# A two-layer hybrid encoder on one core: lo parts by TensorE, a head norm per query, another order of the input projections, and other places for the down projection's operands

## The chip, the cores and the metric

The kernel runs on one core of one Trainium2 chip. The metric is the device time of one execution in microseconds (us), as the median of the runs of a kernel; lower is better.

## What is computed

The reference normalises x (1024 tokens of 1024 features, float32) and sends it through two layers. Cut to what matters, one layer is:

```python
def layer(x):
    proj = x @ w_in + b_in            # conv pair | q | k | v | memory q: 14 chunks of 128, and v of 512
    conv_out = silu(layer_norm(depthwise_conv(a * sigmoid(gate), 31 taps)))    # 256 features
    # 4 differential heads of 128 features, with a relative bias
    s1, s2 = q1 @ k1.T * scale + bias, q2 @ k2.T * scale + bias
    o = (softmax(s1) - lam * softmax(s2)) @ v
    diff_out = o * rsqrt(mean(o * o) + 1e-5) * norm_g * (1 - lam_init)
    mem_out = softmax(qm @ km.T) @ vm                 # 4 heads against 256 memory tokens
    mixed = concat(conv_out, diff_out, mem_out)
    x = layer_norm(ALPHA * x + mixed @ w_out + b_out)
    return layer_norm(ALPHA * x + square(relu(x @ w_up)) @ w_down)   # 4096 hidden features
```

## The kernel before

**Numbers.** Every float32 product is made of two-part operands: a hi part (rounded to the type that TensorE takes, `fp32r` in the trace) and a lo part, the source minus hi. `mm3` (L111) issues three matmuls per product: hi by hi, hi by lo, lo by hi. `split` (L92) makes the parts: hi by a copy on ACT (L97), lo by a subtraction on DVE or POOL (L100). `split_turned` (L199) is the other way to make the parts of a tile that lies in PSUM after TensorE transposed it: ACT copies hi out, TensorE adds `minus` (the negative identity) times hi onto the same PSUM bank, and ACT copies what is left out as lo (L207). Before the change it is used for half of the tiles of the embedding and of the next layer's input (`to_xt`).

**Stages.** The embedding's norm, with the relative bias table and the memory's keys and values for both layers beside it. Then for each layer:

- Input projections (`pj`, L113 to L115) by chunks of 128 columns and halves of 512 tokens, with weights fetched and split by `weight` (L103). The table `ORDER` (L45) gives the order of the steps: letters are chunks (A, gate, Q, K, M), `v` a half of the value projection (`v_ps`), `norm` the transposes `ct` of the convolved channels with their norm (L404), `out` the conv group's silu (`conv_out`, transposes `cz`), `attn:1` the first step of attention. The convolution itself is a chain of scalar_tensor_tensor operations on DVE (`acc`, L344).
- Attention, as a pipeline of 40 blocks of 128 queries in the order of `HEADS`. A block has `scores` (matmuls `sc`, L532; bias and row minimum by DVE, L535; exp by ACT, L537), `combine` (the two softmaxes joined on DVE, L555 to L558), `turn` (8 transposes into two PSUM banks `at`, L578, and the split into tiles `at`), and `values` for pairs of blocks (`o`). In `turn` the first bank of a block is split by ACT and DVE; for the second bank ACT copies the tile out (`av`, L585) and takes hi from that, and POOL makes the lo. After every four blocks of a head comes the head norm: ACT copies `om` out (L619), POOL squares it (DVE in the last head, L621), a 512-column matmul with the 128x128 matrix `ones` sums over the features for all partitions (`ms`, L623), four matmuls add the epsilon term (L626), ACT takes Ln and Exp, and POOL (DVE in the last head) does five operations of 128x512 (L632 to L636).
- Output projection (`wo_ps`, 48 matmuls for each of 8 token tiles), then residual, bias and layer norm (`ln_row`, L149; its statistics by two bn_stats and a bn_aggr on DVE), and the forms `x11`, `x21`, `x22`, `xt1` to `xt4` of the tiles (`turn_form`, L780), which the next stage needs since it multiplies 2x2 blocks by a scheme of 7 products.
- Up projection (`uz`, `uc`, `ud`, L873) with the activation, hidden forms written to DRAM.
- Down projection (`dz`, `db`, L1053): two groups of 7 products, 4 steps (q) in each, 4 token tiles in a step, 6 matmuls for each, 512 columns wide: 2 x 7 x 96 = 1344 matmuls a layer. `down_forms` makes two operands for a step: `wf`, which streams through TensorE, in the stage's own pool `pd`; and `hf`, whose 128x128 parts are loaded as weights, in the pool `wts`. In the last product of group 1 the loaded operand (`hl`) lies in `pd`; in the first product of group 0 the streamed operand of q = 0 and 1 lies in `big`.

**What sets the order.** A scheduler orders the instructions of each engine by their dependencies; the code's order and the pools' buffers bound it. SBUF's pools are stacked from the low end of a partition (`cst`, `big`, `wts`, `sm`, then the stage's pool, `pd` or `pu`) and from the high end (the attention's pools). PSUM has two double banks (`pa`: scores, out projection, half of the down products) and four single ones (`pb`: `at`, `o`, `ms`, `v_ps`, forms, the rest). Loads and stores are issued on SP's queue in order; `bias_rows` (L238) issues four stores of 1 MB that write a skewed copy of each head's bias row (`skew`), from which `attn_load` later reads `bt`. It is called right behind the embedding (L732).

## Time and profile before

| | |
|---|---|
| median of 3 runs | 2481.17 us (2481.14 the lowest) |
| profiled execution | 2482.02 us |
| its span on the core | 2480.2 us, of which PE is busy for 94% |
| embedding, memory keys and values | 0 to 81 us |
| attention of the first layer | 286 to 515 us |
| output projection | 515 to 617 us |
| up projection's start, late forms | 617 to 650 us |
| up projection, then down projection (from 977.5 us) | to about 1240 us |
| second layer's attention | 1484 to 1714 us |

One execution took 9299.67 us; the median is not touched by it. The profile is that of one execution, which took 0.85 us more than the median; 1.8 us of its time lie outside the span. The stages are those of the trace, with their borders read to a microsecond or two.

### The profile page before, as it was taken

Reading aid. Unit: us, or ns where it says so; the run is one execution under the profiler, and the core shown is the slowest. Engines: PE = TensorE matmul, PEld = TensorE weight load, DVE = VectorE, ACT = ScalarE, POOL = GpSimd, SP = SyncE. Lnnn points to the kernel's source line nnn. Section 1 sums busy time; section 2 is a strip of 40 time slices with the busy share of each in tenths; the row PEclk is TensorE's granted clock in tenths of the full one; section 3 lists DMA queues with packets and bytes.
Section 4 is the critical chain, followed back from the end, with each engine's and each line's share of the span. In section 5 each row is a group of like instructions: output and inputs, shape, how many; then the busy total and the mean of one; then the engine's idle time right before and its main releaser. Section 6 shows DMA issues by size and latency. Waiting matters only on the chain.

```text
span 2480.2 us, 30322 instructions
## 1 busy us (share of the span) xinstructions
PE 2321.3 (94%) x11256; PEld 1908.5 (77%) x11256; DVE 1893.9 (76%) x2598; ACT 1105.8 (45%) x1864; POOL 485.0 (20%) x350
## 2 busy tenths in 40 slices
PE   5899998899899999999999899888989999999997
PEld 3788777677688887888878787776768888788885
DVE  7499779969866566757788977897896656586769
ACT  5212387732455554333431137875145555433332
POOL 1124175821000000000042324683200000000002
PEclk9999999999999999999999999999999999999999
DMA  9433445142344449343332346432424444854232
GB/s 315 155 123 98 148 134 146 52 143 106 115 145 145 157 168 398 104 166 97 100 119 85 110 124 194 107 80 92 164 84 139 145 154 152 338 188 161 94 95 101
DMA packets 137740, 355.74 MB, mean 143 GB/s; under 512 B 14804, under 2 KB 31956, under 8 KB 130900
## 3 DMA queue, kind: packets, MB, share of 16 engines
q1 hardware_dynamic: 137592, 353.81, 42.7%
q8 instruction: 88, 1.44, 0.3%
q14 instruction: 60, 0.49, 0.1%
HBM read 240.47 MB, written 117.47 MB: 144 GB/s over the span
## 4 chain that ended last, share of the span: by engine, by line
PE 64%; DVE 27%; issue 4%; DMA 4%; ACT 2%; SPq 0%; DVEq 0%; ACTq 0%
PE uz L873 14%; PE db L1053 12%; PE dz L1053 10%; DVE acc L344 7%; PE uc L873 7%; PE ud L873 4%; DVE s L535 3%; DVE s L557 3%; PE pj L113 2%; PE pj L114 2%; PE pj L115 2%; DVE ast L556 1%; PE wo_ps L115 1%; DVE at L100 1%; PE wo_ps L114 1%
## 5 line engine op out<-in xcount | busy, mean ns | idle before, releaser
L1053 PE MATMUL db<-wf,hf 128*128 128x512 f32 x1344 | 319.6, 398 | 7.0 <-ACT wf L97 5.0
L1053 PEld LDWEIGHTS db<-wf,hf 128*128 128x128 f32 x1344 | 254.9, 190 | 69.1 <-ACT wf L97 6.7
L163 POOL TENSOR_TENSOR yd<-yd,l2g 128x1024 f32<-128x1024 f32 x6 | 14.7, 2442 | 1314.0 <-ACT yd L162 1314.0
L1053 PE MATMUL dz<-wf,hf 128*128 128x512 f32 x1152 | 269.7, 395 | 0.0
L97 ACT ACTIVATE hf<-hr 128x1024 fp32r<-128x1024 f32 x104 | 110.3, 1061 | 337.1 <-PE db L1053 182.3
L1053 PEld LDWEIGHTS dz<-wf,hf 128*128 128x128 f32 x1152 | 217.0, 188 | 50.6
L100 DVE TENSOR_TENSOR hf<-hr,hf 128x1024 fp32r<-128x1024 f32 x104 | 127.1, 1222 | 140.8 <-ACT hf L97 140.2
L97 ACT ACTIVATE wu<-wu_r 128x512 fp32r<-128x512 f32 (+1 forms) x192 | 131.0, 699 | 227.9 <-PE uc L873 95.5
L873 PE MATMUL uz<-xt,wu 128*128 128x512 f32 x768 | 189.8, 395 | 6.0 <-ACT wu L97 6.0
L873 PE MATMUL uz<-x,wu 128*128 128x512 f32 x768 | 191.0, 395 | 0.0
L344 DVE SCALAR_TENSOR_TENSOR acc<-u,pp,acc 128x1009 f32<-128x1009 f32 (+14 forms) x120 | 182.4, 1560 | 0.6
L114 PE MATMUL pj<-x_l,wf 128*128 128x512 f32 x448 | 176.8, 395 | 2.7 <-DVE x_l L100 2.7
L113 PE MATMUL pj<-x_h,wf 128*128 128x512 f32 x448 | 177.3, 397 | 0.4 <-ACT x_h L97 0.4
L100 DVE TENSOR_TENSOR wu<-wu_r,wu 128x512 fp32r<-128x512 f32 (+1 forms) x192 | 145.6, 776 | 39.8 <-ACT wu L97 39.4
L115 PE MATMUL pj<-x_h,wf 128*128 128x512 f32 x448 | 175.9, 393 | 0.0
L873 PEld LDWEIGHTS uz<-xt,wu 128*128 128x128 f32 x768 | 144.1, 188 | 40.3 <-ACT wu L97 6.5
L537 ACT ACTIVATE s<-s,ast 128x1024 f32<-128x1024 f32 x128 | 147.3, 1152 | 55.7 <-DVE ast L535 53.4
L873 PEld LDWEIGHTS uz<-x,wu 128*128 128x128 f32 x768 | 145.9, 190 | 31.8
L535 DVE CUSTOM_DVE_ANT_0 s<-sc,bt 128x1024 f32<-128x1024 f32 x128 | 153.7, 1213 | 10.7 <-PE sc L533 10.0
L100 DVE TENSOR_TENSOR wf<-wd,wf 128x1024 fp32r<-128x1024 f32 x112 | 138.0, 1235 | 26.2 <-ACT wf L97 19.2
L890 DVE TENSOR_TENSOR h<-u,uc 128x512 f32<-128x512 f32 x64 | 44.0, 688 | 144.7 <-PE uc L873 120.8
L532 PE MATMUL sc<-ks,qs 128*128 128x512 f32 x256 | 111.8, 437 | 21.3 <-DVE ast L535 21.1
(261 smaller groups left out, 5365.1 us busy)
## 6 DMA issues: line engine op xcount, KB each, us to landing
hr<-hd SPq DMA_DIRECT2D x224, 256.0 KB, 2.9
wu_r<-in_w_up SPq DMA_DIRECT2D x64, 512.0 KB, 4.2
hd<-hs SPq DMA_DIRECT2D x128, 256.0 KB, 2.4
wd<-in_w_down SPq DMA_DIRECT2D x64, 512.0 KB, 7.7
hd<-h SPq DMA_DIRECT2D x96, 256.0 KB, 2.2
ks<-kd SPq DMA_DIRECT2D x32, 512.0 KB, 11.5
wf_raw<-in_w_f SPq DMA_DIRECT2D x28, 512.0 KB, 4.3
qd<-stg SPq DMA_DIRECT2D x8, 1024.0 KB, 4.4
```

What stands on the lines that cost most here:

```text
L97: nc.scalar.activation(hi, src, AF.Copy)
L100: (lo_eng or nc.vector).tensor_tensor(lo, src, f(hi), op=ALU.subtract)
L113: nc.tensor.matmul(ps, lhsT=lhs[0], rhs=rhs[0], start=start, stop=False)
L114: nc.tensor.matmul(ps, lhsT=lhs[0], rhs=rhs[1], start=False, stop=False)
L115: nc.tensor.matmul(ps, lhsT=lhs[1], rhs=rhs[0], start=False, stop=stop)
L344: nc.vector.scalar_tensor_tensor(acc[:, c, a:b], u[:, c, a + t - PAD:b + t - PAD], pp[:, k:k + 1], acc[:, c, a:b], ALU.mult, ALU.add)
L532: nc.tensor.matmul(ps[:, hf], lhsT=qs[:, m, q], rhs=ks[:, 2 * m, cs], start=True, stop=False)
L535: nc.vector.tensor_tensor_reduce(out=sc[:, m], in0=ps.rearrange("p a b -> p (a b)"), in1=bt[:, b0:b0 + T], scale=-0.125, scalar=3e38, op0= ...
L537: nc.scalar.activation(sc[:, m], sc[:, m], AF.Exp, scale=-1.0, bias=st[:, m:m + 1], accum_out=st[:, 2 + m:3 + m])
L557: nc.vector.scalar_tensor_tensor(sc[:, 0], sc[:, 1], st[:, 5:6], sc[:, 0], ALU.mult, ALU.add)
L873: nc.tensor.matmul(ps, lhsT=a[:, kc], rhs=x[:, c, kc], start=start and kc == 0 and n == 0, stop=stop and kc == 3 and n == 2, skip_group_ch ...
L1053: nc.tensor.matmul(ps, lhsT=h[:, a, n, ts], rhs=w[c][:, n], start=start and n == 0 and m == 0, stop=stop and n == 1 and m == 2, skip_group ...
```

## The change

Six edits, made together:

1. `ORDER`: `norm:0` stands behind `K:1` and `v:1`, where it stood ahead of `K:1`.
2. `BIAS`: the four 1 MB stores of `bias_rows` are issued one by one ahead of the steps `Q:1`, `K:1`, `out:1` and `Q:3` of the first layer, each behind the last weight load issued so far, where they stood behind the embedding.
3. `turn` and `turn_form` use `split_turned`. In `turn` the second bank of each block and both banks of odd blocks get their lo part by TensorE (the first bank of even blocks keeps ACT and DVE). `turn_form` does so for all forms up to `xt1` and for half of the late ones.
4. The head norm: ACT squares `o` out of PSUM, four one-column matmuls give the sum for each query, some ten operations of 128x4 take the inverse root, four matmuls with the identity spread it over the partitions, and one scalar_tensor_tensor on DVE scales `om`.
5. The output projection's layer norm takes its sums on ACT (`stats_act`: a Copy and a Square with accumulation, written to an unused tile).
6. `form_tile`: in the down projection both operands of the steps q = 0 to 2 lie in `pd`, and both of q = 3 in `wts`.

Small tiles change with these: `ones` is one column, `ast` holds four blocks.

```diff
-ORDER = ("first A:1 M:0 M:1 Q:0 K:0 v:0 Q:1 norm:0 K:1 out:0 norm:1 v:1 out:1 close Q:2 K:2 Q:3 attn:1 K:3").split()
+ORDER = ("first A:1 M:0 M:1 Q:0 K:0 v:0 Q:1 K:1 v:1 norm:0 out:0 norm:1 out:1 close Q:2 K:2 Q:3 attn:1 K:3").split()
+BIAS = ["Q:1", "K:1", "out:1", "Q:3"]
...
-    ones = cst.tile([P, P], F32, name="ones")
+    ones = cst.tile([P, 1], F32, name="ones")
...
-    def bias_rows():
-        for h in range(NH):
+    def bias_rows(h):
+        with tc.issue_after(loads[-1].ins):
             nc.sync.dma_start(skew[h].rearrange("(p n) -> p n", n=2049)[:, 0:2048], off8[h:h + 1].to_broadcast([P, 2048]))
...
+            if s in BIAS and l == 0:
+                bias_rows(BIAS.index(s))
...
-                if g == 0 or (h == 0 and qb < 2):
-                    split(at[:, 0, kb, o], at[:, 1, kb, o], pv)
-                else:
-                    av = heads["b"].tile([P, 4, P], F32, tag="av", name=f"av{l}_{h}_{qb}", bufs=2)
-                    nc.scalar.activation(av, pv, AF.Copy)
-                    split(at[:, 0, kb, o], at[:, 1, kb, o], av, nc.gpsimd, nc.gpsimd if qb in (1, 5) else None)
+                split_turned(at[:, 0, kb, o], at[:, 1, kb, o], pt, g or qb % 2)
...
-            eng.tensor_tensor(sq, om, om, op=ALU.mult)
             pm = psum1(f"ms{l}_{h}_{qq}")
-            nc.tensor.matmul(pm, lhsT=ones, rhs=sq, start=True, stop=False)
...
+            for j in range(4):
+                nc.tensor.matmul(pm[:, j:j + 1], lhsT=sq[:, j * P:(j + 1) * P], rhs=ones, start=j == 0, stop=j == 3, skip_group_check=True)
+            e, ln, y, t = (s4[:, :, i] for i in range(4, 8))
+            nc.vector.scalar_tensor_tensor(e, s4[:, :, 2], EPS, s4[:, :, 2], ALU.mult, ALU.mult)
+            nc.vector.tensor_tensor(e, e, pm[:, 0:4], op=ALU.add)
+            nc.scalar.activation(ln, e, AF.Ln)
+            nc.scalar.activation(y, ln, AF.Exp, scale=-0.5)
...
+            for j in range(4):
+                nc.tensor.matmul(pm[:, j * P:(j + 1) * P], lhsT=s4[:, j, 7:8].to_broadcast([P, P]), rhs=ident, start=j == 0, stop=j == 3,
+                                 skip_group_check=True)
+            nc.vector.scalar_tensor_tensor(om, om, lam[:, 3:4], pm, ALU.mult, ALU.mult)
             store_mix(om, mixd, 2 + h, 4 * qq, 4)
...
-            split(xf[name][:, 0, :, cs], xf[name][:, 1, :, cs], pt.rearrange("p (k t) -> p k t", k=4))
+            split_turned(xf[name][:, 0, :, cs], xf[name][:, 1, :, cs], pt, by_pe)
...
-                ln_row(y, g, b, f"l1_{l}_{tb}")
+                ln_row(y, g, b, f"l1_{l}_{tb}", 3, 1, junk)
...
-                turn_form(src, name, t, pu)
+                turn_form(src, name, t, pu, t % 2)
...
+            def form_tile(tag, name, q):
+                if q == 3:
+                    return wts.tile([P, 2, 2, 512], F32R, tag="w8", name=name, bufs=3)
+                return pd.tile([P, 2, 2, 512], F32R, tag=tag, name=name, bufs=3)
...
-                    w = pd.tile([P, 2, 2, 512], F32R, tag="wf", name=f"wf{l}_{gr}_{i}_{q}", bufs=4)
+                    w = form_tile("wf", f"wf{l}_{gr}_{i}_{q}", q)
...
-                if gr and i == PRODS[-1]:
-                    if q % 2 == 0:
-                        wr["h", q // 2] = pd.tile([P, 2, 2, 2, 512], F32R, tag="wd", name=f"hl{l}_{q}", bufs=2)
-                    h = wr["h", q // 2][:, q % 2]
-                else:
-                    h = wts.tile([P, 2, 2, 512], F32R, tag="w8", name=f"hf{l}_{gr}_{i}_{q}", bufs=3)
+                h = form_tile("hf", f"hf{l}_{gr}_{i}_{q}", 3 if not gr and i == PRODS[0] and q < 2 else q)
```

Three places show what moves. In these rows `skew` is the bias store, `wf` a weight of the input projections, `wmk` and `wmv` the memory's, `xres` the residual's store, `bt` the bias read back, and `stg` a projection's result; the digits are layer, chunk and part.

SP's queue at the end of the embedding, before:

```order
L265 DMA wmk1_0_raw_496<-in_w_mk 128x1024
L240 DMA skew0_93<-off8_92 128x2048
L240 DMA skew1_94<-off8_92 128x2048
L240 DMA skew2_95<-off8_92 128x2048
L240 DMA skew3_96<-off8_92 128x2048
L106 DMA wf0_13_raw_1048<-in_w_f 128x1024
L724 DMA xres0_99<-x_5_122 128x1024
L265 DMA wmk1_1_raw_530<-in_w_mk 128x1024
```

The same place in the changed kernel:

```order
L268 DMA wmk1_0_raw_496<-in_w_mk 128x1024
L108 DMA wf0_13_raw_1043<-in_w_f 128x1024
L725 DMA xres0_99<-x_5_122 128x1024
L268 DMA wmk1_1_raw_530<-in_w_mk 128x1024
L725 DMA xres0_99<-x_7_124 128x1024
```

And SP's queue some ten instructions later in the changed kernel, in the input projections:

```order
L108 DMA wv0_0_0_raw_1244<-in_w_v 128x1024
L108 DMA wv0_0_1_raw_1249<-in_w_v 128x1024
L243 DMA skew0_93<-off8_92 128x2048
L487 DMA bt0_0_2042<-skew0_93 128x1920
L373 DMA qmd0_0_645<-stg0_12_1006 128x2048
L108 DMA wf0_5_raw_1503<-in_w_f 128x1024
L243 DMA skew1_94<-off8_92 128x2048
```

The four stores no longer stand ahead of the weights of the memory and of the chunk M:1; the first stands behind the value projection's weights, with the load of `bt` (which reads what it writes) and the weight of Q:1 behind it.

PE in the first layer's input projections, at the first transposes of the convolved channels (`ct`), before:

```order
L113 MATMUL pj0_5_1_1543<-x0_h1_109,wf0_5_1509 128x512
L114 MATMUL pj0_5_1_1543<-x0_l1_110,wf0_5_1509 128x512
L115 MATMUL pj0_5_1_1543<-x0_h1_109,wf0_5_1509 128x512
L404 MATMUL ct0_0_1581<-ident_81,acc0_682 128x128
L113 MATMUL pj0_9_0_1637<-x0_h0_107,wf0_9_1634 128x512
L114 MATMUL pj0_9_0_1637<-x0_l0_108,wf0_9_1634 128x512
L115 MATMUL pj0_9_0_1637<-x0_h0_107,wf0_9_1634 128x512
```

And in the changed kernel:

```order
L115 MATMUL v_ps0_1_7_1852<-wv0_1_1_1645,x0_h1_109 128x256
L116 MATMUL v_ps0_1_7_1852<-wv0_1_1_1645,x0_h1_109 128x256
L117 MATMUL v_ps0_1_7_1852<-wv0_1_1_1645,x0_l1_110 128x256
L409 MATMUL ct0_0_1881<-ident_81,acc0_677 128x128 x8
L115 MATMUL pj0_6_0_2059<-x0_h0_107,wf0_6_2056 128x512
L116 MATMUL pj0_6_0_2059<-x0_l0_108,wf0_6_2056 128x512
```

The transposes now come behind the chunk K:1 (48 matmuls of 512 columns) and the whole second half of the value projection (192 of 256 columns), which followed them before.

DVE at the start of the first layer's attention (`cs` and `cw` are tiles of the conv group's silu, `s` the scores), before:

```order
L424 RECIPROCAL cs0_1_0_2024<-cs0_1_0_2024 128x512
L423 TENSOR_SCALAR cs0_1_1_2033<-cs0_1_1_2033 128x512
L367 SCALAR_TENSOR_TENSOR stg0_10_2147<-pj0_10_1_2150,pp0_651,stg0_10_2147 128x512
L425 TENSOR_TENSOR cw0_1_0_2022<-cw0_1_0_2022,cs0_1_0_2024 128x512
L424 RECIPROCAL cs0_1_1_2033<-cs0_1_1_2033 128x512
L367 SCALAR_TENSOR_TENSOR stg0_7_2208<-pj0_7_0_2183,pp0_651,stg0_7_2208 128x512
L425 TENSOR_TENSOR cw0_1_1_2031<-cw0_1_1_2031,cs0_1_1_2033 128x512
L367 SCALAR_TENSOR_TENSOR stg0_7_2208<-pj0_7_1_2211,pp0_651,stg0_7_2208 128x512
L535 ISA s0_0_0_2239,ast0_0_0_2240<-sc0_0_0_0_2241,bt0_0_2044 128x1024
```

And in the changed kernel:

```order
L541 ISA s0_0_0_2238,ast0_0_0_2239<-sc0_0_0_1_2247,bt0_0_2042 128x1024
L541 ISA ast0_0_0_2239 128x1
L429 RECIPROCAL cs0_1_0_2022<-cs0_1_0_2022 128x512
L541 ISA s0_0_1_2330,ast0_0_0_2239<-sc0_0_1_0_2331,bt0_0_2042 128x1024
L541 ISA ast0_0_0_2239 128x1
L428 TENSOR_SCALAR cs0_1_1_2031<-cs0_1_1_2031 128x512
L541 ISA s0_0_1_2330,ast0_0_0_2239<-sc0_0_1_1_2338,bt0_0_2042 128x1024
L541 ISA ast0_0_0_2239 128x1
L561 RECIPROCAL ast0_0_0_2239<-ast0_0_0_2239 128x1
L430 TENSOR_TENSOR cw0_1_0_2020<-cw0_1_0_2020,cs0_1_0_2022 128x512
L429 RECIPROCAL cs0_1_1_2031<-cs0_1_1_2031 128x512
```

The two reciprocals of the second half of the conv group, which stood ahead of the first scores, now stand between and behind them.

## Rows read from the trace of the kernel before

**Rows 1.** Page, busy time of each engine, and the chain that ended last by line.

```profile
PE 2321.3 (94%) x11256; PEld 1908.5 (77%) x11256; DVE 1893.9 (76%) x2598; ACT 1105.8 (45%) x1864; POOL 485.0 (20%) x350
...
PE uz L873 14%; PE db L1053 12%; PE dz L1053 10%; DVE acc L344 7%; PE uc L873 7%; PE ud L873 4%; DVE s L535 3%; DVE s L557 3%; PE pj L113 2%; PE pj L114 2%; PE pj L115 2%; DVE ast L556 1%; PE wo_ps L115 1%; DVE at L100 1%; PE wo_ps L114 1%
```

**Rows 2.** Windows: from:to, length, busy PE, PEld, DVE, ACT, POOL (count), clock, DMA, GB/s.

```profile
286.00:330.00 44.00, 41.25 (x220) 32.45 (x219) 36.83 (x69) 28.99 (x50) 8.12 (x6) 1.00 0.45 157
...
286.00:515.00 229.00, 200.60 (x1200) 165.08 (x1198) 204.75 (x333) 169.25 (x339) 140.23 (x123) 0.98 0.40 116
...
470.00:515.00 45.00, 35.41 (x207) 27.58 (x207) 43.89 (x68) 31.03 (x54) 26.78 (x18) 0.96 0.23 68
...
561.00:617.00 56.00, 55.18 (x263) 45.52 (x264) 52.33 (x75) 14.78 (x27) 7.21 (x3) 1.00 0.30 104
...
617.00:650.00 33.00, 23.45 (x122) 18.18 (x121) 29.59 (x51) 14.98 (x29) 0.00 (x0) 0.94 0.22 80
...
1484.00:1714.00 230.00, 200.40 (x1200) 166.88 (x1199) 205.01 (x334) 170.34 (x340) 138.62 (x123) 0.97 0.41 117
```

**Rows 3.** Chain in order of time, up and down projection: start, length, what, count.

```profile
907.57 2.72 PE uc L873 x12
910.29 2.79 PE ud L873 x12
...
977.53 22.31 PE dz L1053 x96
```

**Rows 4.** One line's groups, L1053 on PE: least/median/most ns, from first to last.

```profile
L1053 PE MATMUL db<-wf,hl x192: 387/389/499, 1245.1 to 2463.9; 128*128 128x512 f32 x192
...
L1053 PE MATMUL dz<-wf,hf x1152: 390/393/404, 977.4 to 2441.9; 128*128 128x512 f32 x192
```

**Rows 5.** DMA view, 0 to 130 us: count, KB each, us to landing.

```profile
skew<-off SPq DMA_DIRECT2D x4, 1024.0 KB, 16.6
```

**Rows 6.** Page, DMA issues of the whole span: the input projections' weights.

```profile
wf_raw<-in_w_f SPq DMA_DIRECT2D x28, 512.0 KB, 4.3
```

**Rows 7.** Chain in order of time, 0 to 130 us: a weight behind the stores.

```profile
43.81 19.36 DMA wf_raw<-in_w_f
```

**Rows 8.** Waits of PE, 55 to 90 us: total us, times, longest.

```profile
PE km_ps L113 <- ACT wmk L97: 7.6, 1, 7.6
PE vm_ps L114 <- DVE wmv L100: 1.3, 2, 0.8
PE km_ps L115 <- DVE wmk L100: 0.5, 1, 0.5
```

**Rows 9.** Windows, columns as in rows 2: the memory's matmuls behind that wait.

```profile
67.00:81.00 14.00, 12.00 (x73) 11.10 (x74) 5.24 (x8) 3.64 (x7) 3.62 (x2) 0.79 0.73 302
```

**Rows 10.** Waits of PE in the input projections, first layer, then second layer.

```profile
PE ct L404 <- DVE acc L344: 5.5, 2, 4.4
...
PE ct L404 <- DVE acc L344: 5.3, 2, 4.4
```

**Rows 11.** Chain in order of time: a reciprocal of 128x512 on DVE.

```profile
114.50 3.35 DVE e L356
```

**Rows 12.** Groups by line and shape, 286 to 515 us: busy us, mean ns, idle before.

```profile
L557 DVE SCALAR_TENSOR_TENSOR s<-s,ast 128x1024 f32<-128x1024 f32 x32 | 54.2, 1694 | 0.4
...
L100 DVE TENSOR_TENSOR at<-at,at 128x512 fp32r<-128x512 f32 x40 | 27.0, 681 | 0.2 <-ACT at L97 0.2
L97 ACT ACTIVATE at<-at 128x512 fp32r<-128x512 f32 x40 | 23.6, 603 | 11.6 <-PE at L578 11.6
L585 ACT ACTIVATE av<-at 128x512 f32<-128x512 f32 x38 | 22.8, 601 | 0.5 <-PE at L578 0.5
```

**Rows 13.** One line's group, L557 on DVE: least/median/most ns.

```profile
L557 DVE SCALAR_TENSOR_TENSOR s<-s,ast x64: 1267/1285/6114, 293.3 to 1708.0; 128x1024 f32<-128x1024 f32 x64
```

**Rows 14.** Timeline of the embedding: transposes of one bank, and the lo copy that ends it.

```profile
34.20 1.12 PE L196 MATMUL emb_pt<-ident,x 128*128 128x128 f32 x4 [0.84 <-DVE x_l L100]
...
37.22 0.62 ACT L207 ACTIVATE x_l<-emb_pt 128x512 fp32r<-128x512 f32 x1
```

61 lines of the change are left out of this document (26 added, 35 removed).

## The prediction

> **What bounds the kernel now.** I read the page first. PE is busy for 94% of the span, the other engines for 76% and less, and the chain that ended last runs mostly over PE's lines of the up and down projections; but DVE's convolution (`acc`) and attention's score and combine lines stand in it too [rows 1]. So the bulk is bound by PE, and what PE lacks, about 159 us, sits in a few places. Then I cut the span into stages. In the output projection PE is busy for 55.2 of 56 us. In attention it is busy for 200.6 of 229 us, and DVE for 204.8; in attention's last stretch DVE is busy for 43.9 of 45 us and PE for 35.4. The second layer's attention reads the same [rows 2]. So attention is the one long stage where DVE, not PE, ends last. Two smaller holes are named by the waits: one of 7.6 us in the memory's keys [rows 8], and 5.5 and 5.3 us at the convolution's transposes [rows 10]. A saving counts where PE's own matmuls get shorter, or where one of these three places closes.
>
> **Part 1: the down projection's operands.** The chain shows two runs of 12 matmuls of the same shape in the up projection: 2.72 us (226.7 ns each) for `uc` and 2.79 us (232.5 ns) for `ud`. The down projection has 22.31 us for 96, or 232.4 ns [rows 3]. The difference between `uc` and `ud` that I find is the place of the operands: `uc` takes both from `big`, low in SBUF; `ud` streams a late form from the stage's pool above and loads its weights from `big`. In the down projection `wf` streams from `pd`, above, and `hf` is loaded from `wts`, below; in the last product both lie in `pd`, and there the median matmul is 387 to 389 ns where the others have 393 [rows 4]. That is the same step of 4 to 6 ns. Of 2 x 1344 = 2688 matmuls, 192 are `hl` ones and 96 (q = 0 and 1 of the first product) have their streamed part in `big`, which leaves 2400 with operands on two sides. Afterwards, by the pools, all have one side but for those next to a change between `pd` and `wts` and a tile that lies across the border: I take 90. So 2310 x 5.7 ns = -13 us. Bounds: 0, if place is not the cause, and -14, all of them.
>
> By the Trainium skill ("SBUF — State Buffer", section "Who interferes with whom"), PE has independent read ports for the streamed operand and for weight loads and never waits on anyone. By that the two sides would be equal and this part worth nothing; the sum would be 13 us higher. The 5.8 ns between the two up projection runs speak against it, but they are an inference from place alone; it stands as a rival below.
>
> **Part 2: the bias stores.** Four stores of 1 MB take 16.6 us to land [rows 5]. The weight issued behind them takes 19.36 us [rows 7], where the median weight of this kind takes 4.3 [rows 6]. PE then waits 7.6 us for `wmk`, and 1.3 + 0.5 us more for the next lo parts [rows 8]; behind the hole the clock is granted at 0.79 of full speed over 12.0 us of matmuls [rows 9], so some 2.5 us of them are lost. Together 11.9 us. With the stores gone from there, the weights land some 15 us earlier, and all of this should go; the small waits may stay in part, so -11 us (bounds 0 and -12). The stores now go out one at a time among weight loads that have whole chunks as cover. Behind `skew0` the queue holds the load of `bt` until the store has landed, and the weight of Q:1 behind both; its cover is the first half of the value projection. At the 4 us or so that one store alone should take (a quarter of 16.6, an estimate) that is covered; if not, the 12 is given back in part.
>
> **Part 3: the order of the projections.** `ct` moves behind 48 more matmuls of 512 columns (48 x 0.2267 = 10.9 us, by [rows 3]) and the 192 half-width ones (about 22 us), so the 5.5 and 5.3 us [rows 10] go: -10.8 us (bounds 0 and -11). What is late next is `conv_out`, which slips towards attention: its two reciprocals at 3.35 us each [rows 11] now lie among the first scores on DVE. Behind them wait the next score tiles, and behind those PE; 48 matmuls of K:3 stand beside them as cover. I charge +2 us a layer, +4 in all (bounds 0, all covered, and 2 x 2 x 3.35 = +13, none).
>
> **Part 4: attention.** Of 80 banks a layer, 60 now get their lo by TensorE.
> - PE gains 60 x 0.227 = 13.6 us a layer; the norm trades a 512-column matmul for small ones, taken as even. 200.6 + 13.6 = 214.2 us.
> - DVE loses 20 of 40 lo subtractions at 681 ns (13.6 us) [rows 12], and POOL's work of 140 us [rows 2] nearly ends. The combine line has a median of 1285 ns but a mean of 1694 and a maximum of 6114 [rows 12, 13]; I read the excess as stalls beside POOL. Without it 32 x 0.41 = 13 us go. 204.8 - 26.7 = 178 us, so DVE no longer ends last.
> - ACT gains 60 lo copies and loses 38 `av` copies, at about 0.6 us each [rows 12]: +13 us. In the norm it adds a square and drops three passes of 512 columns to two tiny ones, about even. 169.3 + 13 = 182 us.
>
> So PE bounds attention afterwards. At the output projection's share (98.5%) it would take 217.5 us; at the share of attention's first stretch, where DVE was not full either (41.25 of 44, 93.8% [rows 2]), 228.4 us, no gain. Nothing but ACT's turn-around speaks for the second, so I take 219 us, -10 a layer, -20 in all. Bounds: 0, and -57, if the added matmuls fill time that now counts as busy (200.6 us a layer).
>
> **Part 5: output projection and late forms.** The forms by TensorE add about 8 matmuls a layer inside the PE-bound stretch: +1.8 us each. Against that, DVE is relieved of the statistics and of most lo parts, and the 33 us behind the stage, in which PE is busy for 23.45 [rows 2], hold 9.5 us of waiting a layer, DVE busy for 29.6. ACT is busy there for 15 us, and has the room. I take -1.5 a layer net, -3 (bounds +8, with the 16 matmuls a layer at 3.6 us uncovered, and -12).
>
> **Part 6: the layer's end.** The last product now keeps `wts` buffers for q = 3, which delays two of the next layer's first weights. Two splits of 128x1024 at some 2.5 us (twice 0.603 on ACT, 1.285 for a two-input pass of that size [rows 12, 13]) stand against 24 first matmuls (5.4 us): +1 us (0 to +6).
>
> **Sum.** -13 - 11 - 10.8 + 4 - 20 - 3 + 1 = -52.8 us, from the profiled execution's own 2482.0 us: 2429.2 us. The median of the runs lies 0.85 us below that execution, so 2428 us against 2481.2, 2.1% less. About 2% (50 us, so 2431.6) is what a measurement of this kernel can tell from no change.
>
> **The rivals.**
> - *Attention runs into PE's matmuls alone.* DVE's and POOL's relief lets the pipeline close fully: attention at 207 us a layer (half-way to the floor of 200.6), -44 instead of -20, and the late forms at -7: 2401 us. For it: the last stretch, where PE idles for 9.6 of 45 us with DVE full [rows 2]. Against: even the first stretch has 6% of gaps.
> - *The bound moves and attention gains nothing.* Each lo now takes ACT, PE, ACT in turn, and PE's queue is in order, so a `minus` matmul that waits for its hi copy holds the scores behind it. Attention stays at 229 us: 2449 us. For it: ACT's hi copies already waited 11.6 us for PE [rows 12].
> - *The place in SBUF is not what sets 226.7 or 232.4 ns.* Then part 1 does not do what it is read to do here: 2441 us. The rule of the Trainium skill named above ("SBUF — State Buffer", "Who interferes with whom") would have it so. For it: two runs of `uc` and `ud` are one pair of tiles; against it, `hl`.
> - *Slower: PSUM's single banks run out.* A bank in `at` is now held from the transposes to the lo copy: in the embedding 34.20 to 37.84, 3.64 us, with little else on ACT [rows 14]. Attention asks for two banks a block, one every 229 / 80 = 2.86 us; of four, about 1.5 are held by `o` and `ms`. 2.5 free banks carry a hold of 2.5 x 2.86 = 7.1 us; beyond that the block waits for banks. Behind a 24-matmul value product (5.4 us) and an exp on ACT the hold could be 9 us: 7.2 us a block instead of 5.7, +1.5 x 80 = +118 us, with the other parts 2567 us. It decides from 7.1 us on; a hold of 8.3 us already makes the whole slower by 2%. Against: an order of the engines that lets the `minus` matmul stand ahead of the values.
>
> **How the numbers follow.** My forecast 0.45, the first rival 0.2, no gain in attention 0.18, place in SBUF 0.1, banks 0.07. The range takes in the first rival with 11 us beyond it and, above, no gain in attention with part 1 or 3 failing too (2449 + 13 and + 11 are 2460 to 2462) and a few us of part 3's reciprocals: 2390 to 2468; outside are the banks and the tails. Faster by over 2%: the first rival, and a little over half of my own case, 0.48. Slower by over 2%: most of the bank case, 0.05. Within: 0.47.
>
> **What would show it.** Right: `dz` and `db` blocks of 96 at 21.8 us; no wait of `km_ps` for `wmk` near 60 us and an earlier start of `pj`; no `ct` wait; in attention DVE at about 178 us and PE over 95% of the stage. Wrong: `at` or `sc` waits of PE on ACT in place of those on DVE, a wait of `at` for a bank, score tiles late by reciprocals at attention's start, or down blocks still at 22.3 us.

## The result and the profile after

The changed kernel takes 2446.38 us (median of 4 runs, 2442.68 to 2449.0) against 2483.74 us for the kernel before (median of its 4 runs); the ratio is 0.9856, 95% interval 0.9835 to 0.9878. So it is 1.4% faster, clear of no change and within 2% of it. The forecast of 2428 us was 18 us too low; the range held.

Cutting both traces at the first matmul of each stage shows where the 39 us between the two spans (2480.2 and 2440.8 us) come from:

| stage, us | first layer before | after | second layer before | after |
|---|---|---|---|---|
| start, up to the first `pj` | 81.0 | 68.0 | | |
| input projections | 205.2 | 204.4 | 210.2 | 206.5 |
| attention | 229.6 | 229.3 | 229.9 | 229.4 |
| output projection | 101.6 | 98.5 | 101.2 | 98.5 |
| late forms | 32.4 | 30.0 | 32.6 | 30.0 |
| up projection | 293.5 | 288.2 | 293.6 | 288.2 |
| down projection | 330.5 | 331.2 | 323.1 | 323.6 |

Two rows of this table were not foreseen. Attention, on which most of the forecast rested, is as long as before; and the up projection, which no edit was read to touch, lost 5.3 us a layer, while the down projection, which an edit was aimed at, lost nothing. A stage ends here where the first matmul of the next one starts, so work that crosses a border counts on the other side: the last 24 value matmuls (`o`) of attention, about 3 us a layer, ran behind the first `wo_ps` before and run ahead of it after.

The windows of the changed kernel (columns as in [rows 2]): attention of the first and the second layer, then output projection, late forms and up projection of the first.

```profile
272.40:501.70 229.30, 215.27 (x1326) 182.82 (x1325) 180.82 (x336) 180.61 (x376) 36.55 (x42) 0.98 0.41 116
...
1456.20:1685.60 229.40, 213.81 (x1327) 183.26 (x1326) 181.51 (x336) 179.32 (x375) 35.15 (x42) 0.97 0.42 117
...
501.70:600.20 98.50, 98.50 (x461) 80.93 (x460) 61.60 (x88) 42.64 (x78) 14.38 (x6) 1.00 0.39 140
600.20:630.20 30.00, 24.67 (x125) 19.05 (x124) 19.84 (x32) 19.49 (x40) 0.00 (x0) 0.94 0.24 88
630.20:918.50 288.30, 288.30 (x1273) 238.63 (x1273) 182.76 (x270) 153.60 (x258) 0.00 (x0) 1.00 0.48 165
```

Against [rows 2], attention's busy times moved much as worked out: PE 200.6 to 215.3 us (214.2 was forecast; the 24 `o` matmuls from across the border are in the 215.3 and were not in the forecast), DVE 204.8 to 180.8 (178), ACT 169.3 to 180.6 (182). Its length did not follow. PE's share is 93.9%, the share of [rows 2]'s first stretch that the prediction had named as "no gain". The chain of attention, by line, first before, then after:

```profile
by line: DVE s L535 18.9%; DVE s L557 13.3%; issue 8.8%; DVE ast L556 6.5%; DVE at L100 6.1%; DVE ast L558 4.4%; PE sc L532 4.2%; PE sc L533 3.6%; PE o L114 2.7%; PE o L113 2.7%; PE o L115 2.7%; PE at L578 2.7%; ACT s L549 2.2%; DMA kv<-kvd
```

```profile
by line: PE at L199 10.8%; DVE s L541 9.8%; PE sc L538 8.0%; PE sc L539 7.5%; PE o L115 5.8%; PE o L116 5.6%; PE o L117 5.6%; PE at L209 4.3%; DVE s L563 3.3%; issue 3.1%; ACT s L555 3.1%; PE ms L634 2.3%; ACT at L208 2.2%; DMA kv<-kvd 2.1%
```

Before, DVE's lines lead; after, PE's transposes, scores, values and `minus` matmuls (L209) do. The chain moved from one engine to another. PE's longest waits in the first layer's attention after:

```profile
PE sc L538 <- DVE ast L541: 6.2, 10, 1.2
PE at L209 <- ACT at L208: 2.2, 4, 0.7
PE at L199 <- DVE at L102: 1.6, 2, 1.1
```

None is long: 6.2 us in ten pieces for scores behind DVE, 2.2 us for a hi copy ahead of `minus`, 1.6 us for a bank that DVE still reads. All of PE's gaps in this stage come to 14.0 us.

The chain in the up and down projections of the changed kernel, to be held against [rows 3]:

```profile
883.25 2.72 PE uc L873 x12
885.97 2.72 PE ud L873 x12
...
980.53 21.76 PE db L1054 x96
1002.29 21.76 PE dz L1054 x96
```

A block of 96 takes 21.76 us where it took 22.31, as forecast. But `ud` went from 2.79 to 2.72 us too, although its streamed tile still lies in the stage's pool and its weights still in `big`, on two sides. That was the first sign that the side is not the cause. PE's waits in the changed kernel's down projection (910 to 1280 us) show what ate the gain there:

```profile
PE db L1054 <- ACT hf L99: 10.8, 1, 10.8
PE pj L115 <- ACT x_h L99: 1.7, 1, 1.7
```

One wait of 10.8 us at the third step (q = 2) of the first product, where the kernel before waits 3.9 us at the third and fourth step, in four pieces:

```profile
PE db L1053 <- ACT wf L97: 2.9, 2, 2.1
PE db L1053 <- DVE wf L100: 1.0, 2, 0.8
```

ACT's timeline in the changed kernel has most of the reason. PE goes on at 945.73 us, behind the `hf` of 944.62. On ACT's queue that `hf` stands behind a `wf` that waits for its weights until 939.3 us and behind three more copies, and then waits 1.4 us more for a store of hidden forms (`hd`).

```profile
939.30 1.06 ACT L99 ACTIVATE wf<-wd 128x1024 fp32r<-128x1024 f32 x1 [7.75 <-DMA wd<-in_w_down]
940.26 1.04 ACT L99 ACTIVATE hf<-hr 128x1024 fp32r<-128x1024 f32 x1
941.21 1.99 ACT L99 ACTIVATE wf<-wd 128x1024 fp32r<-128x1024 f32 x2
944.62 1.06 ACT L99 ACTIVATE hf<-hr 128x1024 fp32r<-128x1024 f32 x1 [1.42 <-DMA hd<-hs]
```

At the start, the changed kernel's view of DMA (0 to 230 us) and PE's only wait between 45 and 80 us:

```profile
skew<-off SPq DMA_DIRECT2D x4, 1024.0 KB, 6.8
```

```profile
PE km_ps L115 <- ACT wmk L99: 1.0, 1, 1.0
```

The window of 53 to 68 us, in which the memory's matmuls now run:

```profile
53.00:68.00 15.00, 14.51 (x118) 14.31 (x119) 9.06 (x15) 5.88 (x13) 3.62 (x2) 1.00 0.74 283
```

A store of 1 MB now lands in 6.8 us instead of 16.6 [rows 5], the 7.6 us wait of [rows 8] is 1.0 us, and the clock that was granted at 0.79 behind it [rows 9] is granted at 1.00. In the first layer's input projections (81 to 286 us before, 68 to 272 us now) PE waited once for `v_ps` before, beside the `ct` of [rows 10], and now waits like this:

```profile
PE v_ps L113 <- DVE stg L367: 1.2, 1, 1.2
```

```profile
PE v_ps L115 <- DVE stg L370: 3.1, 3, 1.5
PE cz L421 <- DVE z L413: 2.9, 1, 2.9
```

The `ct` wait of [rows 10] is gone; a `cz` wait and a longer `v_ps` wait stand in its place. PE's waits in this stage went from 5.5 + 1.2 = 6.7 us to 3.1 + 2.9 = 6.0 us, which is about the 0.8 us by which the stage got shorter.

### The profile page after: what moved, and what is told of

Same layout as the page of the kernel before. It is cut to its first block, busy times and chain, and to the rows that moved or that the text cites. A ratio compares the mean times of both kernels' runs of the same rounds, so it can differ in the third digit from the quotient of the medians.

```text
span 2440.8 us, 30655 instructions
## 1 busy us (share of the span) xinstructions
PE 2320.9 (95%) x11516; PEld 1937.3 (79%) x11516; DVE 1769.6 (73%) x2516; ACT 1174.7 (48%) x2034; POOL 273.9 (11%) x184
## 4 chain that ended last, share of the span: by engine, by line
PE 77%; DVE 16%; ACT 3%; DMA 3%; issue 2%; SPq 0%; DVEq 0%; ACTq 0%
PE uz L873 14%; PE db L1054 14%; PE dz L1054 10%; PE uc L873 7%; DVE acc L347 7%; PE ud L873 4%; PE wo_ps L117 2%; PE wo_ps L116 2%; PE wo_ps L115 2%; PE at L199 2%; DVE s L541 2%; PE pj L115 2%; PE pj L117 2%; PE pj L116 2%; PE sc L538 1%
## 5 line engine op out<-in xcount | busy, mean ns | idle before, releaser
L1054 PE MATMUL db<-wf,hf 128*128 128x512 f32 x1536 | 357.6, 392 | 22.7 <-ACT hf L99 21.6
L1054 PEld LDWEIGHTS db<-wf,hf 128*128 128x128 f32 x1536 | 289.5, 189 | 85.3 <-ACT hf L99 22.4
L1054 PE MATMUL dz<-wf,hf 128*128 128x512 f32 x1152 | 263.6, 389 | 0.0
L99 ACT ACTIVATE wf<-wd 128x1024 fp32r<-128x1024 f32 x112 | 118.1, 1056 | 272.9 <-PE db L1054 132.4
L99 ACT ACTIVATE hf<-hr 128x1024 fp32r<-128x1024 f32 x112 | 117.3, 1049 | 93.9 <-PE db L1054 41.1
L102 DVE TENSOR_TENSOR hf<-hr,hf 128x1024 fp32r<-128x1024 f32 x112 | 137.0, 1223 | 4.1 <-ACT hf L99 4.1
```

The source lines that it names most:

```text
L99: nc.scalar.activation(hi, src, AF.Copy)
L102: (lo_eng or nc.vector).tensor_tensor(lo, src, f(hi), op=ALU.subtract)
L1054: nc.tensor.matmul(ps, lhsT=h[:, a, n, ts], rhs=w[c][:, n], start=start and n == 0 and m == 0, stop=stop and n == 1 and m == 2, skip_group ...
```

## The experiments

**Side of SBUF, or start address.** In the programs' placement the stage pools above the small tiles (`pu`, `pd`) begin at byte 0x...80 of a 256-byte step in the kernel before, and at 0x...00 in the changed one, because the `ast` tiles take 128 bytes less (the smaller `ones` moves all pools above it by 512). The operands in `big` and `wts` start at 0x...00 in both. Three kernels move that start and keep every operand on its side. The first has smaller `ast` tiles and a pad, so that the pools start at a multiple of 256:

```diff
     sm = pool("sm")
+    sm.tile([P, 32], F32, name="shift")
...
-            st = k["st"] = sm.tile([P, 12], F32, tag="ast", name=f"ast{nm}", bufs=8)
+            st = k["st"] = sm.tile([P, 8], F32, tag="ast", name=f"ast{nm}", bufs=8)
...
-                nc.vector.reciprocal(st[:, 8:12], st[:, 4:8])
+                nc.vector.reciprocal(st[:, 0:4], st[:, 4:8])
```

> The kernel before with one thing changed: the pool above the small tiles starts 128 bytes lower (smaller ast tiles and a pad of 128 bytes), so that the stage pools start at a multiple of 256 bytes and not 128 beside one. The operands stay on the sides they had. Theory 'side' (two sides of SBUF cost 5.7 ns a matmul): nothing moves, dz blocks of 96 stay at 22.3 us, ud at 2.79 us, time within 3 us of before. Theory 'start address' (a streamed tile that starts 128 bytes beside a multiple of 256 costs those 5.7 ns): dz and db blocks at 21.76 us, ud at 2.72, the up projection 5 us a layer shorter, the down projection 5 to 6 us a layer; in all 18 to 26 us less than before.

Measured: 2469.84 us against 2485.21 (ratio 0.9939, interval 0.9918 to 0.9959), 15.4 us less. The chain has its blocks at the lower time, and all groups of the up projection have one median (`ud` had 393 ns before):

```profile
2166.37 21.76 PE dz L1054 x96
2188.13 21.76 PE db L1054 x96
```

```profile
L874 PE MATMUL uz<-xt,wu x768: 389/389/792, 650.2 to 2135.7; 128*128 128x512 f32 x192
L874 PE MATMUL ud<-xt,wu x384: 389/389/628, 651.2 to 2128.9; 128*128 128x512 f32 x192
```

The up projection took 289.5 and 289.9 us, the down projection 326.7 and 318.2 us: 4 us less for the former and 4 to 5 for the latter in each layer. No operand changed its side. The gain is a little under the 18 expected; the effect goes with the start address and not with the side. Its twin differs by the pad alone:

```diff
-    sm.tile([P, 32], F32, name="shift")
```

> The twin of the run before without its pad of 128 bytes: the stage pools start 256 bytes lower than in the kernel before, and so again 128 beside a multiple of 256. Side: as before, 22.3 us for a dz block. Start address: also as before, 22.3 us, ud at 2.79, the whole within 4 us of before.

Measured, in one execution: 2491.15 us, where the kernel before ran from 2482.18 to 2491.87. The chain is back at the old rates, if anything a little above:

```profile
912.64 2.79 PE ud L873 x12
...
977.90 22.40 PE dz L1053 x96
1000.30 22.40 PE db L1053 x96
```

The third puts the pad into the changed kernel, so that its pools start 128 bytes beside:

```diff
     sm = pool("sm")
+    sm.tile([P, 32], F32, name="shift")
```

> The changed kernel with 128 bytes more among the small tiles, so that the stage pools start 128 beside a multiple of 256 again. Side: all as after, since both operands of the down projection stay on one side: dz blocks 21.76 us, up projection 288 us a layer. Start address: the up projection goes back to 293.5 us a layer (+5.3 each); the down projection, whose operands now both start 128 beside, may stay at 21.76 (as hl did before) or go to 22.3; in all 10 to 25 us slower than after.

Measured: 2454.75 us (0.9875 of before, 0.9855 to 0.9896), 8.4 us above the changed kernel's median, a little less than the 10 expected, with intervals that overlap. The chain tells the two stages apart:

```profile
892.06 2.79 PE ud L874 x12
```

```profile
1010.58 21.78 PE dz L1055 x96
1032.36 21.78 PE db L1055 x96
```

`ud` is slow again (up projection 292.3 us a layer), while the down projection, with both operands 128 beside, stays fast. So it is not the absolute start either: in these two stages a matmul is slow when the streamed operand and the weights that are loaded beside it (those of the next matmul) start 128 bytes apart modulo 256, and fast when they start alike. The run itself tells the next matmul's weights from the matmul's own: where the `db` tiles change between `pd` and `wts`, 41 matmuls have streamed operand and own weights alike and the next weights 128 bytes off, and by the programs' addresses and the trace they start 233 ns apart, as slow as the others. That also fits the kernel before, where `hl` and `wf` both started 128 beside and were the fast ones [rows 4]. "Both on one side" is one way to start alike, and an unneeded one.

> The changed kernel with the down projection's operands placed as before (wf in pd, hf in wts, hl in pd). Side: dz blocks go back to 22.3 us, +6 us a layer, while the 10.95 us wait for hf of the first product falls to 4.7: 0 to 2 us faster or slower in all. Start address: blocks stay at 21.76 us and the wait falls to some 4.7 us: 6 us a layer, 12 us faster than after (some 2434 us).

This kernel takes `form_tile` out again and puts the operands where they were:

```diff
-                    w = form_tile("wf", f"wf{l}_{gr}_{i}_{q}", q)
+                    w = pd.tile([P, 2, 2, 512], F32R, tag="wf", name=f"wf{l}_{gr}_{i}_{q}", bufs=4)
...
-                h = form_tile("hf", f"hf{l}_{gr}_{i}_{q}", 3 if not gr and i == PRODS[0] and q < 2 else q)
+                    h = wts.tile([P, 2, 2, 512], F32R, tag="w8", name=f"hf{l}_{gr}_{i}_{q}", bufs=3)
```

Measured: 2439.19 us (0.9822, 0.9798 to 0.9846), 7 us below the changed kernel, with operands on two sides again:

```profile
961.50 21.76 PE dz L1053 x96
983.26 21.76 PE db L1053 x96
```

```profile
PE db L1053 <- ACT wf L99: 6.8, 2, 4.7
PE db L1053 <- DVE wf L102: 0.7, 2, 0.5
```

The blocks stay fast; the wait at the first product falls to 6.8 + 0.7 us, less far than expected, so the down projection gains only 1.5 us a layer in the profiled runs. Edit 6 was not needed for its own end. Whether it cost anything in all is not shown: the medians say 7 us, but the intervals overlap (0.9835 to 0.9878 with it), and the kernel without it has the fast blocks as well.

**Attention.** The next runs stand on that kernel, so they are held against 2439.19 us. Its attention took 234.7 and 232.1 us in the profiled run, and the changed kernel's, with the same code in this stage, 229.3 and 229.4. A third kernel with that code, the one of the output projection below, shows how far one attention can lie from the next (first and second layer of one run):

```profile
271.90:511.10 239.20, 218.78 (x1326) 186.78 (x1325) 185.00 (x336) 181.65 (x376) 36.52 (x42) 0.95 0.41 112
1472.00:1697.20 225.20, 211.86 (x1327) 181.59 (x1326) 177.68 (x336) 178.90 (x375) 35.77 (x42) 0.98 0.42 120
```

The longer one has the clock granted at 0.95 and the shorter at 0.98. So a few us of attention in one profile prove nothing alone; the medians count, and what many runs agree in. First, only the second bank of a block by TensorE:

```diff
-                split_turned(at[:, 0, kb, o], at[:, 1, kb, o], pt, g or qb % 2)
+                split_turned(at[:, 0, kb, o], at[:, 1, kb, o], pt, g)
```

> The kernel of the run with the old places of the down projection's operands, and in attention only the second bank of each block by TensorE (40 of 80 a layer, and 40 by ACT and DVE) where the changed kernel has 60. Theory 'PE bounds attention now': PE loses 20 matmuls of 0.227 us, so 4.5 us a layer, attention 225 us and the whole some 9 us less than with 60. Theory 'the chain from block to block bounds it, whichever engine is busy' : within 3 us of 229 to 234 a layer. Theory 'DVE bounds again at 40': DVE goes from 181 to some 195 us busy of 229, attention 3 us or more longer.

Measured: 2439.89 us, the same; attention 232.1 and 229.2 us in the profiled run, 2.6 and 2.9 us less than its base. DVE is busy for 193.5 us as expected, PE for 212.3, and neither "PE alone" nor "DVE alone" gives what they said. Then none by TensorE, the old `turn`:

```diff
-                split_turned(at[:, 0, kb, o], at[:, 1, kb, o], pt, g or qb % 2)
+                if g == 0 or (h == 0 and qb < 2):
+                    split(at[:, 0, kb, o], at[:, 1, kb, o], pt.rearrange("p (k t) -> p k t", k=4))
+                else:
+                    av = heads["b"].tile([P, 4, P], F32, tag="av", name=f"av{l}_{h}_{qb}", bufs=2)
+                    nc.scalar.activation(av, pt.rearrange("p (k t) -> p k t", k=4), AF.Copy)
+                    split(at[:, 0, kb, o], at[:, 1, kb, o], av, nc.gpsimd, nc.gpsimd if qb in (1, 5) else None)
```

> The same base with attention's turn as in the kernel before (av copies, POOL lo parts), the new head norm kept. If TensorE's lo parts gained the 10 us a layer that the prediction gave them and something else in attention took it back, attention goes to 235 to 240 us a layer. If the edit moved the bound from DVE to PE at no gain, attention stays at 229 to 232 us, DVE at some 195 us busy with its combine line back at a mean of 1.6 us or more.

Measured: 2434.45 us (2434.29 to 2435.3; 0.9792, 0.9777 to 0.9807), 4.7 us less than with 60 banks by TensorE, though the intervals overlap, and attention 225.0 and 227.6 us: shorter than either theory had it, with DVE at 203 us and not at 195. What makes the direction clear is all the runs together: with this `turn` and the new norm, attention took 223 to 228 us in ten layers of five kernels, and with 60 banks by TensorE 225 to 239 us in eight layers of four. The first layer's attention, and the last row with the old head norm as well (the next run):

```profile
272.10:497.10 225.00, 203.95 (x1267) 173.94 (x1265) 202.97 (x357) 167.56 (x345) 94.73 (x89) 0.96 0.42 118
```

```profile
272.00:516.00 244.00, 208.14 (x1224) 173.23 (x1222) 216.36 (x344) 172.95 (x345) 142.53 (x125) 0.95 0.39 109
```

> The same base with both the turn and the head norm as in the kernel before, so that attention is the old one among the other edits. Edits of attention worth nothing: 229 to 232 us a layer, the whole within 5 us of the base. Edits worth what was predicted: 238 us a layer, the whole 16 to 20 us slower than the base.

This run has the old norm's lines (square, 512-column `ones` matmul, five 128x512 operations on POOL) beside the old `turn`:

```diff
-            nc.scalar.activation(sq, pq, AF.Square)
+            eng.tensor_tensor(sq, om, om, op=ALU.mult)
...
+            nc.tensor.matmul(pm, lhsT=full, rhs=sq, start=True, stop=False)
...
+            eng.tensor_tensor(ve, ve, rs, op=ALU.mult)
...
+            eng.tensor_tensor(om, om, ve, op=ALU.mult)
```

Measured: 2459.01 us, 24.6 us more than with the new norm, attention 244.1 and 236.1 us. So the head norm is the part of the attention edits that pays, some 12 us a layer with the old `turn` beside it, clear of noise (0.9863 to 0.9901 against 0.9777 to 0.9807); the lo parts by TensorE cost 2 to 3 us a layer by the medians. But 244 and 236 are also well above the 229.6 us of the kernel before, with the same code in `turn` and norm. About 3 us of that are the 24 `o` matmuls from across the border. Also new in this attention is the conv group's tail, moved there by the new `ORDER`; DVE's groups of this run's attention have it:

```profile
L431 DVE RECIPROCAL cs<-cs 128x512 f32<-128x512 f32 x2 | 6.7, 3338 | 0.0
L430 DVE TENSOR_SCALAR cs<-cs 128x512 f32<-128x512 f32 x2 | 3.0, 1506 | 0.0
L426 DVE TENSOR_SCALAR cw<-cz,pp 128x512 f32<-128x512 f32 x2 | 1.6, 807 | 1.4 <-PE cz L423 1.4
```

Together 11.3 us of DVE, by which DVE's busy time stands 11.6 us above that of [rows 2], in a stage where DVE's lines led the chain. That this tail makes the rest of the difference is likely but not shown: the old attention was not run with the old order, and the clock was granted at 0.95 here.

**Output projection.** Norm sums and forms on DVE again, in the changed kernel itself:

```diff
-        def turn_form(src, name, t, pl=big, by_pe=True):
+        def turn_form(src, name, t, pl=big, by_pe=False):
...
-                ln_row(y, g, b, f"l1_{l}_{tb}", 3, 1, junk)
+                ln_row(y, g, b, f"l1_{l}_{tb}")
...
-                turn_form(src, name, t, pu, t % 2)
+                turn_form(src, name, t, pu, False)
```

> The changed kernel with the output projection's norm sums and all forms' lo parts on DVE again. The prediction's part 5 (net -1.5 us a layer): 1 to 3 us slower. By the traces the output projection went from 101.5 to 98.5 us and the late forms from 32.5 to 30.0 us a layer: if the edits did it, 5 us a layer come back, some 10 us slower than after; if the start addresses did the output projection's part, only the 2.5 us of the late forms come back.

Measured: 2450.65 us, 4.3 us above the changed kernel with an interval (0.9835 to 0.9878 of before) that is the same as that kernel's. The stages are clear where the total is not: the output projection takes 95.5 us instead of 98.5, the late forms 34.4 and 33.7 instead of 30.0, the up projection 290.3 and 289.8 instead of 288.2.

```profile
511.10:606.60 95.50, 95.50 (x446) 78.42 (x445) 73.20 (x102) 20.47 (x38) 14.36 (x6) 1.00 0.40 144
606.60:641.00 34.40, 24.02 (x120) 18.54 (x119) 29.24 (x51) 15.06 (x30) 0.00 (x0) 0.88 0.21 77
```

So norm sums and forms by the new way cost 3.0 us where PE was busy all the time, and gained 4 us behind it. Neither of the two theories: the output projection is not slower without the edits but faster. The total is no measure here: the first layer's attention, which this run does not change, came out 10 us longer than the changed kernel's.

What made the stage shorter than the 101.6 us of before can be read from the traces. Before, PE waits 3.9 us in it (2.9 in the second layer) for the forms and for the stage's first inputs, and the 24 `o` matmuls run in it:

```profile
PE x L780 <- DVE y L170: 2.4, 2, 1.8
PE wo_ps L113 <- ACT ms L97: 1.0, 1, 1.0
PE wo_ps L115 <- DVE ms L100: 0.5, 1, 0.5
```

```profile
515.80:617.40 101.60, 3.18 (x24) 3.07 (x24) 0.60 (x1) 1.00 0.40 138
```

(The last row is the window for the tile `o` alone: PE, PEld and ACT.) In the changed kernel and in this run PE waits for nothing in the stage, and the 24 matmuls are gone from it. That is some 7 us, against the 6.1 us from 101.6 to 95.5. About 3 us of it only crossed the border into attention. The change holds one more edit than the six in its list, which fits this: the loads and splits of the first two token tiles of the output projection's input (`mixed`) are no longer called in the last head's norm, but behind the last `turn`.

```diff
             if h == NH - 1 and qq == 0:
-                ms = big.tile([P, 2, 2, T], F32R, tag="b16", name=f"ms{l}", bufs=4)
-                heads["ms"] = [mixed(l, tb, ms[:, tb], mixd, om) for tb in range(2)]
+                heads["om"] = om
...
                     after(blocks[i - 1])
+                    if i == n:
+                        ms = big.tile([P, 2, 2, T], F32R, tag="b16", name=f"ms{l}", bufs=4)
+                        heads["ms"] = [mixed(l, tb, ms[:, tb], mixd, heads["om"]) for tb in range(2)]
```

The three kernels without it have the 24 matmuls behind the first `wo_ps`, the eleven with it have none there, whichever of the edits to order, `turn`, norm, norm sums and down projection they undo. Only the spread bias stores and the small tiles as changed stand in all eleven beside it. It was not run apart.

**The order of the projections.** On the kernel with the old `turn`, the old table:

```diff
-ORDER = ("first A:1 M:0 M:1 Q:0 K:0 v:0 Q:1 K:1 v:1 norm:0 out:0 norm:1 out:1 close Q:2 K:2 Q:3 attn:1 K:3").split()
+ORDER = ("first A:1 M:0 M:1 Q:0 K:0 v:0 Q:1 norm:0 K:1 out:0 norm:1 v:1 out:1 close Q:2 K:2 Q:3 attn:1 K:3").split()
```

> The run with the old turn (old places of the down operands, new head norm) with the old order of the projections' steps; the bias stores stay spread. Theory 'the ct waits are worth what they show': the input projections get 5 us a layer longer, attention the same, the whole 10 us slower. Theory 'the order only moves the conv group's DVE work into attention': the input projections 0 to 4 us a layer longer, attention 4 to 7 us a layer shorter, the whole 0 to 10 us faster.

Measured: 2429.3 us (2427.63 to 2434.45; 0.9776, 0.9761 to 0.979), 5 us less than with the new order, though the intervals overlap. The input projections are 0.9 and 2.8 us longer, attention 1.8 us longer and 4.7 us shorter. The attention figures lie within the scatter shown above. The `ct` waits of 5.5 and 5.3 us were not worth what they show.

**Two small steps further.** Forms inside the output projection on DVE, but the last tile's and half of the late ones by TensorE:

```diff
-        def turn_form(src, name, t, pl=big, by_pe=True):
+        def turn_form(src, name, t, pl=big, by_pe=False):
...
-            turn_form(q[:, h1], "x22", t)
+            turn_form(q[:, h1], "x22", t, by_pe=t == 3)
...
-            turn_form(q[:, h0], "xt1", t)
+            turn_form(q[:, h0], "xt1", t, by_pe=t == 3)
```

> The run with the old turn, with the forms made inside the output projection (x11, x21, x22, xt1 of all tiles but the last) on DVE again, the last tile's and half of the late forms still by TensorE, the norm sums still on ACT. If TensorE's forms cost what their matmuls take inside a stage that PE bounds, the output projection goes from 98.5 to 95.5 us a layer and the late forms stay at 30: 6 us faster. If DVE's backlog comes back, the late forms go to 34 us and the whole moves by less than 3 us.

Measured: 2432.42 us. The output projection takes 95.9 us, the late forms 30.7 and 30.9: 1.8 us a layer, as the first theory has it but for 1 us of late forms; the total, 2.0 us less, does not tell it from no change. And the tiles stacked from the top of SBUF moved by 128 bytes, with which, by the programs' addresses, all but two dozen of the output projection's 768 and of attention's 608 512-column `sc` matmuls start alike:

```diff
-    pool("edge", side="right").tile([P, 24], F32, name="edge")
+    pool("edge", side="right").tile([P, 56], F32, name="edge")
```

> The run with the old turn, with 128 bytes more at the top of SBUF, so that the pools stacked from there (wo, k, s of attention's start) also start at a multiple of 256 bytes. Theory 'the streamed operand and the next weights must start alike modulo 256 bytes': 480 out-projection matmuls and some 230 score matmuls gain 5.7 ns each, the output projection 1.3 us a layer shorter, 2 to 5 us in all. Theory 'only the stage pools above the weights matter': no change, within 1.5 us.

Measured: 2433.24 us (2426.95 to 2436.93), which alone tells nothing; but the output projection takes 97.2 us in both layers where it took 98.5, the 1.3 us of the first theory (some 230 matmuls of 5.7 ns):

```profile
497.00:594.20 97.20, 97.20 (x461) 80.75 (x460) 62.84 (x89) 42.81 (x79) 14.34 (x6) 1.00 0.40 144
1678.30:1775.50 97.20, 97.20 (x462) 80.82 (x461) 61.14 (x87) 42.59 (x78) 14.33 (x6) 1.00 0.39 139
```

The other half of that theory failed. The score matmuls, 227 of which started 128 bytes apart and now start alike, did not get faster (the base first, then this run):

```profile
L538 PE MATMUL sc<-ks,qs x256: 387/397/796, 272.1 to 1657.3; 128*128 128x512 f32 x128
```

```profile
L538 PE MATMUL sc<-ks,qs x256: 387/397/776, 272.0 to 1658.3; 128*128 128x512 f32 x128
```

In the kernel before too, score matmuls that start alike take 393 ns by the median, like those that do not. What holds them at that rate was not tried.

**All that did not lose, together**: the edits of the runs with the old `turn`, the old order, the forms and the `edge` of 56, in one kernel.

> Everything that did not lose, together: the changed kernel with the old places of the down operands, the old turn, the old order of the projections' steps, the forms inside the output projection on DVE, and 128 bytes more at the top of SBUF; kept from the change are the spread bias stores, the new head norm, the norm sums on ACT, late forms by TensorE and the small tiles that let the stage pools start at a multiple of 256. Additive theory, from the three runs against the one with the old turn (2434.45): -5 for the order, -2 for the forms, -1 to -3 for the right side: 2424 to 2427 us. Theory 'the order's gain was attention's own scatter of a few us from run to run': 2428 to 2433 us.

Measured: 2424.86 us (2423.57 to 2429.13; 0.9761 of before, 0.9748 to 0.9775), inside the additive theory's range: 21.5 us below the changed kernel and 2.4% below the kernel before. Attention takes 225.0 and 224.0 us, the output projection 94.4 us a layer.

## Why the prediction was right, and where its steps failed

The direction and the range were right, the size was 37 instead of 53 us, and what came about looks like the second rival (the bound moves, attention gains nothing, 2449 us). That 2446 lies so near to 2449 is in part luck: the rival keeps all other parts as forecast, and they were off in both directions; and its mechanism, scores held behind a `minus` matmul that waits for its hi copy, shows in no more than 2.2 us of waits.

- **Part 1, the down projection's operands (-13 us).** The size of the effect was right (22.31 to 21.76 us a block), its cause and its place wrong. "The difference between `uc` and `ud` that I find is the place of the operands" is the step that failed: the two also differ in their start modulo 256 bytes, and the runs with and without 128 bytes decide for that. What shifted the pools was the smaller `ast` tiles, an accident of the change. So the up projection, priced at nothing, gave 10.7 us, and the down projection lost its own gain to a wait that was not priced. In the changed kernel the third `hf` of the first product lies in `pd`, and on ACT it stands behind a `wf` that waits for its load; with the old places the wait is on `wf` alone and 3 us shorter. Why those loads and stores end when they do was not tried.
- **The rule that was weighed there.** By the Trainium skill ("SBUF — State Buffer", "Who interferes with whom") PE has independent read ports for the streamed operand and for weight loads, and never waits on anyone. The third rival, drawn from that, has the side without effect, which is so; but equal rates are not: 2.79 and 2.72 us for the same twelve matmuls, moved at will by 128 bytes. Rule and measurement differ, and the measurement decides.
- **Part 2, the bias stores (-11 us): right.** The start is 13.0 us shorter, the small waits went too, and so did the lost clock. The cover held although a store takes 6.8 us and not the 4 of the estimate. The stores alone were not run apart.
- **Part 3, the order (-10.8 and +4 us).** The waits went as said, but the input projections lost only 0.8 and 3.7 us. The step that failed is taking the wait for the worth: `conv_out` moved back with `ct`, a `cz` wait of 2.9 us and `v_ps` waits came up. Whether the tail on DVE weighed on attention by the 2 us a layer charged, by more or by nothing, the runs do not tell: with the new norm and the old `turn`, the old order made attention 1.8 us longer in one layer and 4.7 us shorter in the other.
- **Part 4, attention (-20 us): wrong.** Busy times were forecast within 3 us, PE's with some luck, since the 24 `o` matmuls were not in the sum; "at the output projection's share" was the step that failed. The stage stayed at the share of its first stretch. It was also one sum for two edits of opposite sign: by the runs, the head norm is worth about -12 us a layer while the old `turn` stands beside it, the lo parts by TensorE +2 to +3 by the medians, and about 3 us of `o` matmuls came in from the output projection. What took the rest stays open; the order's tail is a likely part. Why TensorE's lo parts lose, with DVE relieved by 22 us, is shown only so far that the chain passes to PE's lines; which wait of it decides was not isolated.
- **Part 5 (-3 us): under-sized.** It gave 5.5 us a layer: 2.4 to 2.6 us of late forms, and 2.7 to 3.1 us in the output projection, where a loss of up to 3.6 us had been feared. That loss is there (3.0 us). It lies under a gain that was not foreseen: the waits of 3.9 and 2.9 us that the stage had before, and the `o` matmuls that left it. The sum had neither, since the 55.2 of 56 us that it went by are those of the stage's second half.
- **Part 6** was too small to be told apart. **The slower rival**, PSUM's banks, did not come: the wait for a bank that a lo part still holds is the 1.6 us shown.

## What to carry to other kernels

When two runs of the same matmul differ by a few nanoseconds, list everything in which their operands differ, and move one of it by a pad that does nothing else: here 128 bytes were worth 15 us, and the edit aimed at the effect had the wrong cause. A wait in the trace is worth its length only if no other wait comes up in its place: here 6.7 us became 6.0. Where one edit adds work to an engine and another takes work off, price and run them apart. And when stages are compared, count whether the same work lies in them: 24 matmuls that crossed a border shifted about 3 us from one stage to the other.

## What the runs showed of the hardware that was not expected

For the 512-column matmuls of this kernel's up, down and output projections, the streamed operand and the weights loaded beside it want the same start modulo 256 bytes: in the down projection 21.76 to 21.78 us for 96 where they start alike, both at a multiple or both 128 beside, and 22.31 to 22.40 us where they differ by 128, whichever side of SBUF they lie on. Other differences than 0 and 128 hardly occur here. The score matmuls of attention do not follow: they keep the slower rate when they start alike.
